# The last tile of a second up projection by seven block products, and where its activations are parted

## The chip, the cores and the metric

The kernel runs on one core of one Trainium2 chip. The metric is device time in microseconds (us), from one launch that computes the whole block. Three runs of the kernel before gave 1013.27, 1013.62 and 1014.18 us; the median is 1013.62 us.

## The reference, cut to what matters

One layer of a streaming encoder on 512 frames of width 1024: a SwiGLU feed-forward network (FFN) with half a step, a token mixer, and a second FFN with half a step. Everything is fp32. The change lies in the second FFN:

```
D_MODEL, SEQ, D_FF = 1024, 512, 2816

def _swiglu(h, w_in, w_out):
    gate, up = jnp.split(h @ w_in, 2, axis=-1)
    return (jax.nn.silu(gate) * up) @ w_out

h = _modulate(x, sh3, s3)
x = x + 0.5 * g3[:, None, :] * _swiglu(h, ffn2_w_in[l], ffn2_w_out[l])
```

The two factors of width 2816 of the up projection, gate and up, are worked in 22 tiles of 128 columns; each tile gives 128 rows of the activation silu(gate) * up, held transposed as 128 partitions by 512 frames.

## The kernel before, in words

**Numbers in two parts.** To keep fp32 accuracy on fp32r matmuls every operand is split into a high part (a cast by ScalarE, ACT) and a low part (a subtraction by VectorE, DVE). A product takes three matmuls: high by high, high by low, low by high (`mm3`, L473). Weights are split by `split_w` (L233, called through `halved`): one cast (L234) and one subtraction (L235) for a tile of 128x1024. Activations are split by `glu_parts` (L915): one cast (L918) and one subtraction (L919) of 128x512. In this text an activation that has been split is "parted".

**Plain tiles.** A plain tile of the up projection (in `by_sevens`, from L1009) takes two weight units, gate and up, each with 8 k-steps of three matmuls of 512 columns: 48 matmuls. `glu` (L907) then applies silu, multiplies and parts the result.

**Tiles by block products.** `seven_products` (L344) computes gate and up of one tile together as a 2x2 block product with seven half-size products in place of eight. Each product is 4 k-steps of three matmuls of 256 columns: 84 matmuls. The order is 1, 2, 6, 7, 5, 4, 3; between them ACT copies partial sums out (L365, L370, L373, L377) and applies silu in two halves (L374, L384), DVE makes three additions (L363) and the last multiplication (`self.mul`, its instruction at L1444). The sums of the inputs (`t7`) are made once; the sums of the weights are made for each tile by `sevenths` (L270): on ACT three casts of 128x1024 and one of 128x512, on DVE three subtractions of 128x1024 and five operations of 128x512. That preparation of tile f+1 is put beside the products of tile f: `side.step()` stands at five places in `seven_products`, and `side.flush()` does the rest after it.

**The second FFN.** `ffn2` (L1263) makes tiles 0 to 2 plainly. `by_sevens` (L974) is called with `SEVEN[1]` = tiles 3 to 20. Then its loop at L1009 makes tile 21 plainly. A generator `parted()` (L1002) parts activations 0 to 7 and 16 to 20 (8 to 15 are in `left` and are parted later); `side.step(3)` at four places beside tile 21 issues twelve of these thirteen. Activations 16 to 21 go to a pool `late` of 12 buffers that takes over the memory of the pool `seven` when the last block product is done (`late_exit`, `late_enter`). A second generator that runs slowly beside the sevens (`ada_more`, 0.12 steps for each step of the first) ends with four matmuls (L885), a copy of their result `rw` (L888) and four transposes (L892).

**The down projection.** `last_down` (L1119) goes through `PLAN`: two heads (output tiles 0 and 1, activations 0 to 7, 24 matmuls of 512 columns each), three tails (activations 16 to 21, 18 matmuls each), three pairs of output tiles by seven block products over activations 0 to 7 (`seven_down`, L1192), five tails, and four pairs over activations 8 to 15. Before matmuls on an activation that isn't parted, it steps the same generator (`self.splits`, L1172). Beside the heads and tails it makes the sums of the activations for the block products (`act_sums`, L1098, instructions at L1102 and L1439, L1440) from the unparted activations 0 to 7 in `self.whole`.

**What sets the order.** The framework fills the queue of each engine ahead of time: among instructions whose inputs it expects to be ready it takes the one that stands first in the program, so work may be drawn ahead into a gap. Three things hold it back. `queued` (L184) ties all ACT instructions issued within it into one chain in the order of the program; the block at L993 holds `seven_products` and `side.flush()`, and the chain goes on from tile to tile. Buffers of one pool and tag (56 in `slots`, four each of `wr`, `wh` and `wl` for weights) are given out in the order in which their first writers stand in the program. And a weight tile's buffers are free only after the matmuls that read them. A load of weights (L139, on the queue of SyncE, SP) starts when its raw buffer `wr` is free; `preload(2)` at L992 calls for the next two loads one tile before the last of the sevens.

Of the kernel before, what the change touches and what calls it, by code (L numbers as in the profile page):

```python
# [25 lines left out]
FT = DFF // P  # L26
EPS = 1e-6
HALF = NT // 2
KPARTS = ((0, 8), (8, 8), (16, 6))
SEVEN = range(6, 21), range(3, 21)  # L30
PAD = 112
SEVENS = 0, 1
PLAN = (("head", 0), ("head", 1), ("tail", 0), ("tail", 1), ("tail", 2), (0, 2), (0, 4), (0, 6), ("tail", 3), ("tail", 4),
# [66 lines left out]
class Block:  # L100
# [325 lines left out]
    def plan_units(self):  # L426
# [4 lines left out]
        def ffn(w1, w2, first, plan, seven=()):  # L431
            for f in range(first, FT):
                if f in seven:
                    self.specs.append(lambda f=f: self.unit_pair(w1, f * P))
                    continue
                cols(w1, f * P)
                cols(w1, DFF + f * P)
            for kind, t in plan:
                if kind in SEVENS:
                    self.specs.append(lambda t=t, k0=8 * kind: self.unit_rows(w2, t, k0))  # L440
                    continue
                for k0, n in (part for i, part in enumerate(KPARTS) if i not in MISSING[kind]):
                    self.specs.append(lambda k0=k0, n=n, t=t: self.unit(w2[k0 * P:(k0 + n) * P, t * P:(t + 1) * P], n))

        ffn(ins["ffn1_w_in"][0], ins["ffn1_w_out"][0], 3, [("all", t) for t in range(KT)], SEVEN[0])
        w = ins["w_in"][0]
# [9 lines left out]
        first = len(self.specs)  # L456
        ffn(ins["ffn2_w_in"][0], ins["ffn2_w_out"][0], 0, PLAN, SEVEN[1])
        del self.specs[first:first + 3]
# [478 lines left out]
    def ffn1(self):  # L937
# [14 lines left out]
        sums.flush()  # L952
        self.by_sevens(act, SEVEN[0], (self.ada_more((1, 2, 3), accs, 0),), 0.3)
        return act
# [19 lines left out]
    def by_sevens(self, act, fs, others, rate, left=()):  # L974

        side, other, self.last_queued = Side(), Side(), None
        other.add(*others)
        both = Rates((side, other), (1, rate))

        def first():  # L980
            yield
            yield
            self.prefetch(1)

        for f in fs:
            w = self.weights7
            if f + 1 in fs:
                side.add(self.next_unit(ahead=0))
            else:
                side.add(first())  # L990
            if f + 2 == fs.stop:
                self.preload(2)  # L992
            with self.queued(mybir.EngineType.Activation, self.last_queued):  # L993
                act.append(self.seven_products(w, both))
                side.flush()
        other.flush()
        self.late_exit()
        self.late_enter(12)
        last = fs[-1] + 1
        self.whole = act[:8]  # L1000

        def parted():  # L1002
            for i in range(last):
                if i not in left:
                    act[i] = self.glu_parts(act[i], i >= 16 if left else 8 <= i < 14)
                    yield

        side.add(parted())
        for f in range(last, FT):  # L1009
            p = []  # L1010
            for _ in range(2):
                u, q = self.next_unit(), self.acc()
                for k in (0, 4):
                    self.dense(q, u, self.h, k0=k, k1=k + 4)
                    side.step(3)
                p.append(q)
            act.append(self.glu(*p, late=bool(left)))
        self.splits = side
# [244 lines left out]
    def ffn2(self, norms):  # L1263
# [13 lines left out]
        side.flush()  # L1277
        self.by_sevens(act, SEVEN[1], (self.ada_more((12, 13), [], 3),), 0.12, range(8, 16))
        self.last_down(act, 8)
# [1209 lines left out]
```

## Time and profile before

| | before |
|---|---|
| median of three runs | 1013.62 us |
| profiled execution, its own time | 1014.92 us |
| its span, first to last instruction | 1013.1 us |
| granted TensorE clock over the span | 0.999 |
| instructions on TensorE (PE) | 7101 matmuls, 7101 weight loads |
| bytes moved by DMA | 130.84 MB, 129 GB/s on the mean |
| DMA engines busy, mean of 16, share of the span by the q1 queue | 42.2% |

A row of the timeline gives the start in us from the start of the span, how long the instruction (or a run of like ones) took, the engine, the line, the operation, the tiles written and read (buffer numbers left out), shapes, the count, and in brackets the idle time of the engine just before it with what ended it. A row of the stages gives the stretch, its length, then the busy time and number of instructions of PE matmul, PE weight load, DVE, ACT and POOL, then the granted clock, the DMA share and GB/s. Matmuls overlap one another, so what one costs in a row of many is the distance between starts, not its own duration.

### The profile page before, as it was taken

What the parts mean: (1) busy time and instruction counts of PE and PEld (TensorE: products, weight loads), DVE (VectorE), ACT (ScalarE), POOL (GpSimd) and SP (SyncE); (2) the same over time, 40 slices, a digit from 0 to 9 for tenths busy, and PEclk for the clock granted to TensorE, in tenths of its full rate; (3) what the DMA queues carried; (4) which work ended last, traced back from release to release, by engine and by line L of the source; (5) the groups of instructions that cost most, each with busy time, mean ns of one, the idle gap of its engine ahead of it and who ended that gap; (6) DMA issues with size and microseconds to landing.
All of it is one profiled execution on the core that took longest, in us unless ns stands there. A gap on an engine that the chain in (4) does not pass through costs nothing.

```text
span 1013.1 us, 18031 instructions
## 1 busy us (share of the span) xinstructions
PE 1001.7 (99%) x7101; PEld 907.7 (90%) x7101; DVE 822.0 (81%) x1461; ACT 527.2 (52%) x954; POOL 30.7 (3%) x74
## 2 busy tenths in 40 slices
PE   7999999999999999999999999999999999999998
PEld 5788999999887889888887888999999999989898
DVE  4778999887797847788987649789998998799984
ACT  4355555556422215658766455375555555655453
POOL 0000000000200000100001012000000000000000
PEclk9999999999999999999999999999999999999999
DMA  9963564434598925412132121212544443323332
GB/s 312 295 208 104 165 208 137 117 102 122 155 323 281 306 65 156 111 47 58 46 75 57 39 63 43 83 43 75 175 121 150 121 131 105 110 83 91 113 104 63
DMA packets 204034, 130.84 MB, mean 129 GB/s; under 512 B 14497, under 2 KB 188590, under 8 KB 203950
## 3 DMA queue, kind: packets, MB, share of 16 engines
q1 hardware_dynamic: 203950, 129.70, 42.2%
q8 instruction: 55, 0.90, 0.4%
q14 instruction: 29, 0.24, 0.1%
HBM read 127.18 MB, written 2.49 MB: 128 GB/s over the span
## 4 chain that ended last, share of the span: by engine, by line
PE 89%; DVE 5%; DMA 2%; SPq 1%; ACT 1%; issue 1%; POOL 0%; DVEq 0%; ACTq 0%
PE pa L360 18%; PE pa L475 14%; PE pa L477 13%; PE pa L476 13%; PE pb L360 13%; PE pa L1207 4%; PE pb L1207 3%; SPq L139 1%; DMA ar<-in_w_ada 1%; PE pb L2175 1%; PE pb L2155 1%; PE pb L475 1%; PE pb L477 1%; PE pb L476 1%; DMA wr<-in_ffn_w_in 1%; PE pb L1712 1%
## 5 line engine op out<-in xcount | busy, mean ns | idle before, releaser
L275 DVE TENSOR_TENSOR wl<-wr,wh 128x1024 fp32r<-128x1024 f32 x120 | 145.8, 1220 | 26.8 <-ACT wh L279 25.8
L279 ACT CAST wh<-wr 128x1024 fp32r<-128x1024 f32 x120 | 123.1, 1051 | 32.9 <-DVE wr L275 18.9
L234 ACT CAST wh<-wr 128x1024 fp32r<-128x1024 f32 (+1 forms) x77 | 76.8, 1006 | 116.8 <-PE pa L476 109.4
L475 PE MATMUL pa<-hh,wh 128*128 128x512 f32 (+1 forms) x309 | 119.4, 386 | 0.0
L235 DVE TENSOR_TENSOR wl<-wr,wh 128x1024 fp32r<-128x1024 f32 (+1 forms) x77 | 89.3, 1165 | 33.4 <-ACT wh L234 33.3
L477 PE MATMUL pa<-hh,wl 128*128 128x512 f32 (+1 forms) x309 | 116.2, 376 | 0.0
L476 PE MATMUL pa<-hl,wh 128*128 128x512 f32 (+1 forms) x309 | 116.1, 376 | 0.0
L475 PE MATMUL pa<-ah,wh 128*128 128x512 f32 (+1 forms) x262 | 97.9, 374 | 0.0
L476 PE MATMUL pa<-al,wh 128*128 128x512 f32 (+1 forms) x262 | 97.5, 372 | 0.0
L477 PE MATMUL pa<-ah,wl 128*128 128x512 f32 (+1 forms) x262 | 97.3, 371 | 0.0
L275 DVE TENSOR_TENSOR wr<-wr,wr 128x512 f32<-128x512 f32 x120 | 82.4, 687 | 1.7
L828 DVE SCALAR_TENSOR_TENSOR aa<-ar,sc,aa 128x512 f32<-128x512 f32 x98 | 73.3, 748 | 8.0 <-DMA ar<-in_w_ada 6.5
L360 PE MATMUL pa<-th,wh 128*128 128x256 f32 x264 | 74.8, 283 | 0.0
L360 PE MATMUL pa<-hh,wh 128*128 128x256 f32 x264 | 74.8, 283 | 0.0
L360 PE MATMUL pa<-tl,wh 128*128 128x256 f32 x264 | 74.7, 283 | 0.0
L360 PE MATMUL pa<-th,wl 128*128 128x256 f32 x264 | 74.7, 283 | 0.0
L360 PE MATMUL pa<-hl,wh 128*128 128x256 f32 x264 | 74.7, 283 | 0.0
L360 PE MATMUL pa<-hh,wl 128*128 128x256 f32 x264 | 74.7, 283 | 0.0
L475 PEld LDWEIGHTS pa<-hh,wh 128*128 128x128 f32 x309 | 58.4, 189 | 10.9 <-issue 2.5
L477 PEld LDWEIGHTS pa<-hh,wl 128*128 128x128 f32 x309 | 58.2, 188 | 10.1
L476 PEld LDWEIGHTS pa<-hl,wh 128*128 128x128 f32 x309 | 58.4, 189 | 8.5
L475 PEld LDWEIGHTS pa<-ah,wh 128*128 128x128 f32 x262 | 49.3, 188 | 10.2 <-ACT wh L234 1.7
(484 smaller groups left out, 2769.1 us busy)
## 6 DMA issues: line engine op xcount, KB each, us to landing
wr<-in_ffn_w_in SPq DMA_DIRECT2D x79, 512.0 KB
ar<-in_w_ada SPq DMA_DIRECT2D x128, 256.0 KB
wr<-in_ffn_w_out SPq DMA_DIRECT2D x32, 512.0 KB
wr<-in_w_in SPq DMA_DIRECT2D x21, 512.0 KB
wr<-in_ffn_w_out SPq DMA_DIRECT2D x16, 384.0 KB
wr<-in_w_out SPq DMA_DIRECT2D x8, 512.0 KB
wr<-in_ffn_w_in SPq DMA_DIRECT2D x8, 384.0 KB
ar<-in_w_ada SPq DMA_DIRECT2D x6, 512.0 KB
```

The source lines that it names most:

```text
L139: return self.nc.sync.dma_start(dst, src)
L234: self.nc.scalar.copy(hi, raw)
L235: self.nc.vector.tensor_tensor(out=lo, in0=raw, in1=hi.bitcast(F32), op=ALU.subtract)
L275: sub = lambda out, x, y: nc.vector.tensor_tensor(out=out, in0=x, in1=y, op=ALU.subtract)
L279: nc.scalar.copy(hi[:, :n], raw[:, :n])
L360: nc.tensor.matmul(z, a[:, j, :], b, start=start and j == 0 and i == 0, stop=j == 3 and i == 2, skip_group_check=not start)
L475: mm(out, wh, xh, start=start, stop=False)
L476: mm(out, wh, xl, start=False, stop=False)
L477: mm(out, wl, xh, start=False, stop=stop)
L828: nc.vector.scalar_tensor_tensor(out=acc, in0=a, scalar=sc, in1=acc, op0=ALU.mult, op1=ALU.add)
L1207: nc.tensor.matmul(z, a[:, j, :], b, start=start and j == 0 and i == 0, stop=j == 3 and i == 2, skip_group_check=not start)
L1712: nc.tensor.matmul(pa[:, ps], kh[:, ps], x[:, ps], start=True, stop=True)
```

## The change

`SEVEN[1]` now ends at tile 21 instead of 20, so the second FFN makes all of tiles 3 to 21 by block products, and `plan_units` loads the weights of tile 21 as one pair (the same two loads of 512 KB). The loop for plain tiles after the sevens finds nothing to do. During tile 21 a generator `begin()` is added to the side work behind `first()`: it yields three times and then parts activations 0 to 3. `first()` yields twice and then splits the weights of head 0. `self.whole` is set before that, because `begin()` replaces entries of `act`. `parted()` skips what is parted already and is left with activations 4 to 7 and 16 to 21; `last_down` steps it. The first FFN calls the same function with tiles up to 20 and keeps its order.

```
-SEVEN = range(6, 21), range(3, 21)
+SEVEN = range(6, 21), range(3, FT)
...
+        def begin():
+            for _ in range(3):
+                yield
+            for i in range(4):
+                act[i] = self.glu_parts(act[i])
+                yield
+
         for f in fs:
             w = self.weights7
...
             if f + 2 == fs.stop:
                 self.preload(2)
+            if f + 1 == FT:
+                self.whole = act[:8]
+                side.add(begin())
             with self.queued(mybir.EngineType.Activation, self.last_queued):
                 act.append(self.seven_products(w, both))
                 side.flush()
...
-        self.whole = act[:8]
+        if last < FT:
+            self.whole = act[:8]
 
         def parted():
             for i in range(last):
-                if i not in left:
+                if i not in left and not isinstance(act[i], tuple):
                     act[i] = self.glu_parts(act[i], i >= 16 if left else 8 <= i < 14)
                     yield
```

## The prediction, made before the changed kernel was run

> **What bounds the kernel now.** I read the page first, then the stages around the change, then the timelines of PE, DVE and ACT there.
>
> ```profile
> span 1013.1 us, 18031 instructions
> PE 1001.7 (99%) x7101; PEld 907.7 (90%) x7101; DVE 822.0 (81%) x1461; ACT 527.2 (52%) x954; POOL 30.7 (3%) x74
> ```
>
> Over the whole span TensorE (PE) hardly ever rests. The stages tell more: tile 19, tile 20, tile 21 with what precedes it, the two heads and three tails, three pairs by block products, five tails, and the first pair of the second set.
>
> ```profile
> core 0: us, PE busy (x) PEld busy (x) DVE busy (x) ACT busy (x) POOL busy (x), PEclk, DMA share, GB/s
> 858.02:868.10 10.08, 10.08 (x87) 10.08 (x86) 8.47 (x13) 5.55 (x10) 0.00 (x0) 1.00 0.37 104
> 868.10:878.18 10.08, 10.08 (x86) 10.03 (x84) 4.85 (x8) 5.25 (x10) 0.00 (x0) 1.00 0.39 108
> 878.18:890.88 12.70, 12.70 (x59) 9.51 (x57) 11.76 (x19) 8.94 (x17) 0.00 (x0) 1.00 0.51 147
> 890.88:914.00 23.12, 23.12 (x104) 19.14 (x102) 21.92 (x39) 11.09 (x16) 0.00 (x0) 1.00 0.23 67
> 914.00:924.08 10.08, 10.08 (x86) 10.08 (x85) 9.71 (x17) 6.03 (x11) 0.00 (x0) 1.00 0.31 94
> 924.08:934.16 10.08, 10.08 (x87) 10.08 (x86) 9.99 (x17) 6.30 (x11) 0.00 (x0) 1.00 0.26 78
> 934.16:944.24 10.08, 10.08 (x87) 10.08 (x86) 9.73 (x18) 5.98 (x11) 0.00 (x0) 1.00 0.60 171
> 944.24:964.66 20.42, 20.42 (x93) 16.89 (x91) 20.13 (x35) 8.89 (x12) 0.00 (x0) 1.00 0.28 80
> 964.66:974.74 10.08, 10.08 (x84) 10.00 (x83) 9.19 (x13) 4.95 (x8) 0.00 (x0) 1.00 0.39 116
> ```
>
> PE is busy in every microsecond of these stages. But from 878 to 965 DVE is too: 9.71 to 9.99 of 10.08 us in the pairs, 20.13 of 20.42 in the five tails. It keeps up only because it is some microseconds ahead. Tile 20 is the last place with room on DVE (4.85 of 10.08), because the plain tile behind it needs little preparation.
>
> **What the change takes from PE.**
>
> ```profile
> 868.10 0.28 PE L360 MATMUL pa<-hh,wh 128*128 128x256 f32 x1
> ...
> 878.27 1.05 PE L885 MATMUL pb<-aa,ones 128*32 128x512 f32 x4
> 879.25 0.50 PE L475 MATMUL pa<-hh,wh 128*128 128x512 f32 x1
> ...
> 890.88 0.39 PE L475 MATMUL pa<-ah,wh 128*128 128x512 f32 x1
> ...
> 896.32 0.39 PE L475 MATMUL pa<-ah,wh 128*128 128x512 f32 x1
> ...
> 968.97 0.28 PE L1207 MATMUL pb<-th,wh 128*128 128x256 f32 x1
> ```
>
> A block-product tile is 84 matmuls in a stage of 10.08 us (858.02 to 868.10): 0.120 us each. Head 0, 24 matmuls from 890.88 to 896.32, gives 0.2267 us for one of 512 columns, so 48 of a plain tile take 10.88 us. PE saves 0.80 us. The four matmuls of L885, 1.07 us of PE from 878.18 to 879.25, stay: the slow generator is one step further in the new tile 21, so they move to between products 6 and 7; their transposes come behind the tile. SP's loads are the same in number and size, and in the same places.
>
> The Trainium skill's page "TensorE: Matmul & The Clock Gate", section "Back-to-back issue gap", gives N/2.4 + 2.5 ns for one matmul, 109 and 216 ns here; by that 84 against 48 would save 1.19 us. The rows above say 120 and 227 ns, and the rows decide.
>
> **What it adds to DVE, and where.** These are DVE's rows from the end of tile 19 to the start of tile 21, and two from later:
>
> ```profile
> 869.38 0.68 DVE L1444 TENSOR_TENSOR af<-sg,up 128x512 f32<-128x512 f32 x1
> 871.25 0.42 DVE L363 TENSOR_TENSOR sg<-pb,z 128x256 f32<-128x256 f32 x1 [1.19 <-PE pb L360]
> 875.71 1.22 DVE L235 TENSOR_TENSOR wl<-wr,wh 128x1024 fp32r<-128x1024 f32 x1 [4.04 <-ACT wh L234]
> 876.86 0.42 DVE L363 TENSOR_TENSOR up<-z 128x256 f32<-128x256 f32 x1
> 877.19 0.42 DVE L363 TENSOR_TENSOR up<-pb,z 128x256 f32<-128x256 f32 x1
> 877.52 2.35 DVE L235 TENSOR_TENSOR wl<-wr,wh 128x1024 fp32r<-128x1024 f32 x2
> 879.79 0.68 DVE L1444 TENSOR_TENSOR af<-sg,up 128x512 f32<-128x512 f32 x1
> ...
> 891.15 0.69 DVE L912 TENSOR_TENSOR af<-sg,pa 128x512 f32<-128x512 f32 x1 [0.96 <-PE pa L477]
> 891.75 0.42 DVE L1102 TENSOR_TENSOR t<-af 128x256 f32<-128x256 f32 x1
> ...
> 965.75 1.23 DVE L275 TENSOR_TENSOR wl<-wr,wh 128x1024 fp32r<-128x1024 f32 x1
> ```
>
> *Work.* In steady state a tile costs DVE 8.47 us, of which its own three additions (0.33 from start to start) and one multiplication (0.60) are 1.6; the preparation of the next pair is thus 6.9, which I round down to 6.7 as runs of instructions overlap. Added: 6.7 for pair 21 and 1.0 for tile 21's three additions. Removed: two weight splits, 1.15 each from start to start. Multiplication and parting of activation 21 cost the same. Net +5.4 us.
>
> *Room.* Tile 20 becomes a steady tile: DVE works 8.47 and idles 1.61 where it idled 5.23. In the new tile 21 there is nothing to prepare but the weights of heads and tails, and they can't begin early: head 0's cast is in ACT's chain behind product 7's copy and silu, and the buffers of head 1's and tail 0's follow its in the program. In the old tile 20 the cast at that place and its subtraction stand at 874.64 (quoted below) and 875.71. One stage of 10.08 and L885's 1.07 later that subtraction starts at 886.86. DVE has finished tile 20 at 869.38 + 0.68 + 10.08 = 880.14, does one addition (0.42), and idles 6.3 us.
>
> Could parting fill this? `begin()` yields three times behind the three steps of `first()`, and there are five steps in a tile; all four partings therefore come in the flush, behind the last silu in ACT's chain. Those of activations 4 to 7 and the sums L1102 wait for buffers of the pool `slots`, given out in program order, so behind those of 0 to 3, which are behind activation 21's own. The trace shows this order holding work back: the sum at 891.75 needs only activations made long before, yet DVE idles 0.96 us for L912, whose buffer comes first. Activations 16 to 20 wait for the pool `seven` to end, after product 4. The old plain tile had none of this: it held DVE busy 11.76 of 12.70 us with partings.
>
> ```profile
> 868.30 0.38 ACT L384 ACTIVATE sg<-pa 128x256 f32<-128x256 f32 x1 [0.61 <-PE pa L360]
> ...
> 874.64 1.04 ACT L234 CAST wh<-wr 128x1024 fp32r<-128x1024 f32 x1
> ...
> 879.95 0.63 ACT L918 CAST ah<-af 128x512 fp32r<-128x512 f32 x1
> ```
>
> *At the border.* The four casts are not beside tile 21, then, but behind it, and head 0 waits for the first. The silu starts 0.20 us after the tile's last matmul slot (868.10 to 868.30) and takes 0.38; the cast takes 0.63; together 1.2 us, less about 0.5 for the transposes that PE has there: 0.7 us. The low part needs one multiplication and one subtraction of 0.6 to 0.7 on DVE more; PE can draw head 1's first matmul in. I price the wait at 0.7 to 1.9. Alone it would leave -0.8 + 1.3 = +0.5 us.
>
> *The account to the end of DVE's busy stretch.* The work that decides last is the subtraction at 965.75, ending at 966.98: it is read by product 7 of the first pair of the second set, whose matmuls start at 968.97. DVE is 2.0 us ahead there. Idle of DVE from 868.10 to 964.66 by the stages: 5.23 + 0.94 + 1.20 + 0.37 + 0.09 + 0.35 + 0.29 = 8.5 us. After: 1.6 + 6.3, and of the 2.3 us behind 890.88 what is left. The 0.96 us wait at 891.15, and a few others for PE, go once DVE is the late one; I take 0.3, between 0 and 2.3. DVE is then later by 5.4 + 8.2 - 8.5 = 5.1 us, 2.0 are covered, and PE has to wait until **+3.1 us**. This holds the border wait and the 0.8 saved: PE waits 3.9 in all, part of it at the border, the rest in products 6 and 7 of the pairs. Behind 974.74 nothing is given back, since PE is busy throughout. With the idle left at 0 and 2.3 the sum is 2.8 and 4.8; if half the 2.0 us lead can't be used, 1.0 more; if the sums of the work are 1.0 too high or the framework draws work behind this subtraction, 1.0 less.
>
> The profiled execution took 1014.92 us, 1.8 more than its span and 1.30 more than the median. I add 3.1 to span (1016.2) and median alike: **1016.7 us**. A measurement of this kernel tells about 0.2%, 2.0 us, from no change.
>
> **Rivals.**
>
> *PE alone decides: faster by 0.8 to 0.9.* PE is busy 99%, so what it saves is saved. The Trainium skill's page "Perfetto Trace Analysis", section "Identifying the Most-Contended Engine", has it so: the engine with the highest occupancy is the one to improve. For it: PE doesn't wait once between 868 and 975 now. Against it: the stages show DVE at 96 to 99% over 30 us, and DVE gets 5.4 us more. It would need 3 us of partings within DVE's 6.3 us gap, which the chain and the buffer order forbid. 1012.8 us; chance 0.10.
>
> *Only the border wait counts.* The account is 2.5 us too high because the framework, finding DVE late, sets work back that PE doesn't need before 975 (updates of xT, later partings), or because DVE's lead is larger than the one row shows. Then -0.8 + 1.0 to 2.3: +0.2 to +1.5, 1014.2 us at +0.6; chance 0.25.
>
> *DVE's debt decides*: the forecast, slower than before, from the point where the debt (5.1) is over the lead (2.0). 1016.7, between 1015.6 and 1018.4; chance 0.57.
>
> *The heads starve as well.* If ACT and DVE alternate between activations 0 to 7 and 16 to 20, an activation comes every 1.2 us (twice 0.60) while head 0 eats one in 0.68 (3 x 0.2267). If PE's queue can't interleave head 1, eight of them cost 8 x 0.52 = 4.2 us on top of the 1.2: +4.6, 1018.2 or a little over; chance 0.05.
>
> *The change doesn't do what it says* in the sense that nothing is parted beside the tile: that is in the forecast. Its opposite, four partings (2.4 us) in the gap, would bring the debt to 2.7 and the end to about +0.7, within the second rival. A gain of over 2.0 us has no mechanism that I can find: 0.03.
>
> **How the numbers follow.** Slower by over 0.2% takes most of the forecast (0.55 of its 0.57) and the starving heads: 0.60. Within 0.2%: 0.37. Faster: 0.03. The range 1013.4 to 1018.5 leaves out the first rival below and the worst of the last one above. The forecast's own range is 1015.6 to 1018.4.
>
> **What would show it.** Right: in tile 21 DVE busy under half of the first 8 us; the casts of activations 0 to 3 directly behind the last silu; PE's first wait at head 0, 0.7 to 1.9 us; more PE waits, for DVE's weight subtractions or sums, in the first four pairs; no difference in any tile before 868. Wrong: DVE subtractions L919 in the gap of tile 21; no PE wait in the pairs; head 0 starting without a wait; a span that differs before 868.

## The result, and the profile after

The changed kernel takes 1017.81 us (median of 15 runs, 1015.88 to 1020.36); the kernel before, on the same chip in turn with it, 1014.51 us (median of 15 runs, 1013.21 to 1018.07). The ratio is 1.0032, with a 95% interval of 1.0025 to 1.0039: slower by about 3.3 us.

The first part of the page of the changed kernel has the span and each engine's busy time:

```profile
span 1018.5 us, 18100 instructions
PE 1004.1 (99%) x7137; PEld 910.8 (89%) x7137; DVE 826.3 (81%) x1470; ACT 529.9 (52%) x961; POOL 30.6 (3%) x74
```

PE, DVE and ACT look as they did. The execution that was profiled took 1020.36 us, the longest of the fifteen, so its times are for reading the mechanism, and the medians for its size. The stages tell where it went. The seven rows are those that the prediction shows of the kernel before (tile 19, tile 20, tile 21, heads and tails, three pairs, five tails, first pair of the second set), except that the three pairs stand in one row; the eighth is the first 8 us of tile 21.

```profile
core 0: us, PE busy (x) PEld busy (x) DVE busy (x) ACT busy (x) POOL busy (x), PEclk, DMA share, GB/s
858.75:868.83 10.08, 10.08 (x87) 10.08 (x85) 8.46 (x13) 5.56 (x10) 0.00 (x0) 1.00 0.37 104
868.83:878.91 10.08, 10.08 (x87) 10.08 (x85) 8.45 (x13) 5.55 (x10) 0.00 (x0) 1.00 0.36 106
878.91:891.91 13.00, 11.79 (x94) 10.55 (x92) 6.59 (x11) 7.52 (x15) 0.00 (x0) 1.00 0.32 93
891.91:917.54 25.63, 25.16 (x103) 20.31 (x103) 23.97 (x46) 12.73 (x22) 0.00 (x0) 0.93 0.28 82
917.54:949.65 32.11, 30.95 (x254) 30.46 (x252) 32.11 (x53) 19.34 (x35) 0.00 (x0) 1.00 0.33 97
949.65:970.08 20.43, 20.43 (x93) 16.90 (x91) 19.75 (x38) 9.57 (x14) 0.00 (x0) 1.00 0.35 101
970.08:980.16 10.08, 10.08 (x86) 10.08 (x85) 9.57 (x15) 5.17 (x9) 0.00 (x0) 1.00 0.38 106
878.91:886.91 8.00, 8.00 (x63) 7.03 (x62) 2.40 (x4) 2.58 (x7) 0.00 (x0) 1.00 0.34 99
```

Tile 21 with its border is 0.30 us longer (12.70 before), heads and tails 2.51 (23.12), the three pairs 1.88 (30.23). Behind the pairs nothing changes: five tails 20.43 against 20.42, the first pair of the second set 10.08 both times. The remaining 0.73 us lies before tile 21 (878.91 against 878.18), and all of it already before tile 19 (858.75 against 858.02); PE's instructions up to there are the same, and executions vary by as much (in the control of the experiments, whose edit lies behind 914, the plain tile 21 starts at 878.35, in the kernel before at 879.25).

PE's waits from 860 to 1010, grouped by the instruction that waited and the one that released it, as total, count and longest; in the kernel before this view is empty:

```profile
PE pa L475 <- ACT ah L918: 1.2, 1, 1.2
PE pa L1218 <- DVE wl L275: 0.7, 1, 0.7
PE pa L476 <- DVE al L919: 0.5, 1, 0.5
PE pb L1218 <- ACT wh L279: 0.4, 1, 0.4
```

Four waits, at two places. The first place is the border of tile 21 and head 0, in PE's timeline:

```profile
890.25 0.46 PE L892 MATMUL pb<-ident,rw 64*128 64x64 f32 x4
891.91 0.73 PE L475 MATMUL pa<-ah,wh 128*128 128x512 f32 x2 [1.21 <-ACT ah L918]
893.11 0.50 PE L476 MATMUL pa<-al,wh 128*128 128x512 f32 x1 [0.46 <-DVE al L919]
...
893.92 0.59 PE L476 MATMUL pa<-al,wh 128*128 128x512 f32 x1
894.32 0.63 PE L477 MATMUL pa<-ah,wl 128*128 128x512 f32 x1
...
897.30 0.43 PE L475 MATMUL pa<-ah,wh 128*128 128x512 f32 x1
```

Head 0 waits for the high part of its first activation, does the two matmuls that it can, and waits again for the low part. Then its matmuls come 0.43 us apart (894.32, 894.74, ...) in place of 0.23. The stage view of just that stretch gives the granted clock:

```profile
893.92:897.30 3.38, 3.38 (x9) 2.61 (x8) 3.38 (x7) 3.38 (x8) 0.00 (x0) 0.50 0.95 284
```

Half the clock for 3.4 us costs this execution 1.6 us (eight matmuls at 0.2 us more). It isn't in every execution. Of the fifteen runs, seven have a mean clock of 0.999 or 1.0 and a median of 1017.08 us; the eight with 0.997 or 0.998 have 1018.54.

The second place is the first of the three pairs, in PE's timeline:

```profile
917.54 0.28 PE L1218 MATMUL pa<-ah,wh 128*128 128x256 f32 x1
...
921.39 0.38 PE L1218 MATMUL pb<-th,wh 128*128 128x256 f32 x1 [0.44 <-ACT wh L279]
...
925.49 0.39 PE L1218 MATMUL pa<-ah,wl 128*128 128x256 f32 x1 [0.72 <-DVE wl L275]
```

And DVE's weight subtractions there, in the kernel after and then in the kernel before:

```profile
920.16 1.23 DVE L275 TENSOR_TENSOR wl<-wr,wh 128x1024 fp32r<-128x1024 f32 x1
...
921.96 1.21 DVE L275 TENSOR_TENSOR wl<-wr,wh 128x1024 fp32r<-128x1024 f32 x1
...
924.22 1.21 DVE L275 TENSOR_TENSOR wl<-wr,wh 128x1024 fp32r<-128x1024 f32 x1
```

```profile
911.10 2.35 DVE L275 TENSOR_TENSOR wl<-wr,wh 128x1024 fp32r<-128x1024 f32 x2
...
915.10 1.23 DVE L275 TENSOR_TENSOR wl<-wr,wh 128x1024 fp32r<-128x1024 f32 x1 [0.15 <-ACT wh L279]
```

The first two are the later weights of pair 1 (for products 5 and 6, then 7 and 3), the third is the first weights of pair 2. Before, the two were ready when the pairs began at 914.00 (911.10 + 2.35 = 913.45), and DVE itself waited for ACT ahead of the third. After, all three come while the pair runs, one behind the other. The PE row at 925.49 is a matmul of pair 2: the framework had drawn it in among those of pair 1, and in PE's queue it holds up all behind it. In the kernel before it was not drawn in. There the same matmul comes behind all of pair 1, 10.31 us after the pairs' start:

```profile
924.31 0.28 PE L1207 MATMUL pa<-ah,wl 128*128 128x256 f32 x1
```

The third subtraction sums the matter up in one number. Let its **lag** be its end less the start of the pairs: 915.10 + 1.23 - 914.00 = 2.33 us before, 924.22 + 1.21 - 917.54 = 7.89 after. The experiments below are read by it.

### The profile page after: what moved, and what is told of

Read it like the earlier page. It is cut to its first block, busy times and chain, and to the rows that moved or that the text cites. A ratio compares the mean times of both kernels' runs of the same rounds, so it can differ in the third digit from the quotient of the medians.

```text
span 1018.5 us, 18100 instructions
## 1 busy us (share of the span) xinstructions
PE 1004.1 (99%) x7137; PEld 910.8 (89%) x7137; DVE 826.3 (81%) x1470; ACT 529.9 (52%) x961; POOL 30.6 (3%) x74
## 5 line engine op out<-in xcount | busy, mean ns | idle before, releaser
L275 DVE TENSOR_TENSOR wl<-wr,wh 128x1024 fp32r<-128x1024 f32 x123 | 149.1, 1219 | 26.8 <-ACT wh L279 25.9
L279 ACT CAST wh<-wr 128x1024 fp32r<-128x1024 f32 x123 | 125.7, 1051 | 25.9 <-DVE wr L275 21.5
L235 DVE TENSOR_TENSOR wl<-wr,wh 128x1024 fp32r<-128x1024 f32 (+1 forms) x75 | 86.9, 1163 | 36.0 <-ACT wh L234 35.8
L475 PE MATMUL pa<-hh,wh 128*128 128x512 f32 (+1 forms) x293 | 113.0, 386 | 0.0
L477 PE MATMUL pa<-hh,wl 128*128 128x512 f32 (+1 forms) x293 | 110.0, 375 | 0.0
L476 PE MATMUL pa<-hl,wh 128*128 128x512 f32 (+1 forms) x293 | 109.9, 375 | 0.0
L360 PE MATMUL pa<-th,wh 128*128 128x256 f32 x272 | 77.1, 283 | 0.5 <-ACT z L365 0.5
L475 PEld LDWEIGHTS pa<-hh,wh 128*128 128x128 f32 x293 | 55.4, 189 | 9.5 <-issue 1.6
L477 PEld LDWEIGHTS pa<-hh,wl 128*128 128x128 f32 x293 | 55.2, 188 | 9.6
L476 PEld LDWEIGHTS pa<-hl,wh 128*128 128x128 f32 x293 | 55.4, 189 | 7.9
```

Source lines behind the costliest of these rows:

```text
L235: self.nc.vector.tensor_tensor(out=lo, in0=raw, in1=hi.bitcast(F32), op=ALU.subtract)
L275: sub = lambda out, x, y: nc.vector.tensor_tensor(out=out, in0=x, in1=y, op=ALU.subtract)
L279: nc.scalar.copy(hi[:, :n], raw[:, :n])
L360: nc.tensor.matmul(z, a[:, j, :], b, start=start and j == 0 and i == 0, stop=j == 3 and i == 2, skip_group_check=not start)
L475: mm(out, wh, xh, start=start, stop=False)
L476: mm(out, wh, xl, start=False, stop=False)
```

## The experiments

Ratios are against the kernel before, run in turn on the same chip, with 95% intervals; each kernel was executed 5 to 12 times. "Waits" are by how much the starts of neighbouring matmuls on PE lie further apart than 0.120 us (0.227 for 512 columns), summed over 905 to 935, or the part of it where it says so. Theory A is the forecast's: DVE is late by its added work and by the gap in tile 21, and PE pays what is over DVE's lead.

**Four partings inside tile 21.** The three empty steps of `begin()` go, it calls for head 0's weights itself, and `first()` isn't added for the last tile, so that activations 0 to 3 are parted within tile 21 and not behind it.

```
         def begin():
-            for _ in range(3):
-                yield
             for i in range(4):
+                if i == 2:
+                    self.prefetch(1)
                 act[i] = self.glu_parts(act[i])
                 yield
...
-            else:
+            elif f + 1 < FT:
                 side.add(first())
```

> The changed kernel, but the four partings of activations 0 to 3 are issued at steps 1 to 4 inside tile 21 (head 0's weights still split at step 3), so they can run in DVE's idle stretch there. Theory A (DVE's debt): the border wait goes, and 2.4 us of DVE's work moves into the idle stretch; debt 5.1 to 6.5 less 2.4, less the lead of 2.0: +0.7 to +2 us against the kernel before; waits in the first pair by block products stay. Theory B (only the wait at head 0 and the half clock behind it cost): nothing is left but PE's saving, -0.8 us.

Measured: 1016.28 us, ratio 1.0020 (1.0011 to 1.0029). Head 0 starts at 890.21, right behind L892: the border wait is gone, and with it the half clock. The waits in the first pair grew, to 2.4 us from 1.8. Two of them:

```profile
917.36 0.39 PE L1218 MATMUL pa<-th,wh 128*128 128x256 f32 x1 [0.55 <-ACT wh L279]
...
918.62 0.38 PE L1218 MATMUL pb<-th,wh 128*128 128x256 f32 x1 [0.75 <-ACT wh L279]
```

Measured from the start of tile 20, and against the run without `begin()` below (the changed kernel without the half clock), PE came to the pairs 1.8 us earlier and DVE to the end of the third subtraction only 1.4, so the lag rose to 8.37. Of the 1.7 us of border wait 0.6 was paid in the pairs. That the border is the whole loss is refuted; the 2.0 us that are left lie at the upper end of what A gave.

**Eight partings inside tile 21.** The same with two at each of four steps.

```
         def begin():
-            for _ in range(3):
-                yield
-            for i in range(4):
-                act[i] = self.glu_parts(act[i])
+            for step in ((0, 1), (2, 3), (), (4, 5), (6, 7)):
+                if not step:
+                    self.prefetch(1)
+                for i in step:
+                    act[i] = self.glu_parts(act[i])
                 yield
...
-            else:
+            elif f + 1 < FT:
                 side.add(first())
```

> As the last one, but eight partings (0 to 3 at steps 1 and 2, 4 to 7 at steps 4 and 5 of tile 21). Theory A: 4.8 us of work in the idle stretch, the debt is 0.3 to 1.7 and under the lead of 2.0, so only PE's saving is left: -0.8 us against the kernel before (between -1.2 and +0.3). Theory B: the same -0.8, no better than with four.

Measured: 1013.55 us, ratio 0.9992 (0.9983 to 1.0000), the lowest ratio of the study, with an interval that reaches to no gain. DVE's idle time in tile 21 falls from 6.4 to 3.9 us, the border wait is gone, and the lag is down to 7.07 us. One wait of 0.95 us with its restart is left, for that same subtraction:

```profile
919.68 0.39 PE L1219 MATMUL pa<-ah,wl 128*128 128x256 f32 x1 [0.69 <-DVE wl L275]
```

That wait eats what PE saves. From the start of tile 20 to the first pair of the second set PE takes 96.77 us here and 96.56 in the kernel before, so the trace doesn't show the median's gain at the place of the change. The same stretch is 101.25 us in the changed kernel, and 99.76 in the next run, which had no half clock.

**No `begin()`.** No partings are added beside tile 21; `parted()` does all of them behind it.

```
-                side.add(begin())
```

> The changed kernel without begin(): all fourteen partings are left to the generator that the heads step. Theory A: no difference from the changed kernel, +3.3 us against the kernel before (+2.5 to +4), because activation 21's buffer and DVE's work are the same. Theory C (ACT's chain holds the four casts, the rest doesn't matter): the casts come free and start earlier; +1 us or less.

Measured: 1017.10 us, ratio 1.0028 (1.0018 to 1.0037), as the changed kernel. The same four waits, of the same lengths (1.21, 0.46, 0.44, 0.72 us), and a lag of 7.90. The four partings "beside" the last tile are not beside it: the generator does nothing that its absence wouldn't.

**Plain tile, four partings.** The kernel before, with one parting a step in place of three beside its plain tile 21 (the calls share this line; the first FFN keeps three).

```
-                    side.step(3)
+                    side.step(1 if left else 3)
```

> The kernel before with a plain tile 21, but four partings beside it in place of twelve: the second half of the change alone. Theory A: eight partings, 4.8 us of DVE, move behind the tile, where DVE has 2.0 us of lead: +1.5 to +3 us against the kernel before. Theory D (the block products of tile 21 and their preparation are what costs): within 0.5 us of the kernel before.

Measured: 1014.23 us, ratio 1.0001 (0.9991 to 1.0010). A expected 1.5 us or more and missed; the rival, that only the block products' preparation costs, held here. The lag is 6.24, and PE waits 0.1 us. So DVE's lead was larger than the 2.0 us of the forecast.

**DVE's work alone, in three doses.** The kernel before, with the low-part subtraction of some activations repeated, which adds work to DVE and nothing else.

```
-        nc.vector.tensor_tensor(out=al[:, ts], in0=a[:, ts], in1=ah[:, ts].bitcast(F32), op=ALU.subtract)
+        for _ in range(1 + again):
+            nc.vector.tensor_tensor(out=al[:, ts], in0=a[:, ts], in1=ah[:, ts].bitcast(F32), op=ALU.subtract)
```

> The kernel before with three of these subtractions (activations 5 to 7) made twice: 1.8 us more on DVE. Theory A: under the lead of 2.0 us and DVE's small idle stretches, so no cost, -0.3 to +0.5 us against the kernel before. A bound without any lead would give +1.8 us.

> The kernel before, with nine of the low-part subtractions of parting (activations 3 to 7 and 16 to 19) made twice: 9 x 0.6 = 5.4 us more on DVE beside the old tile 21 and the heads, and nothing else. Theory A (DVE's debt over a lead of 2.0 us): +1.5 to +3.4 us against the kernel before, with PE waits for DVE at the first pairs by block products. Theory B (only the wait at head 0 and the half clock behind it cost): 0 to +0.5 us.

Measured: three repeats, 1014.78 us, ratio 1.0005 (0.9996 to 1.0014); nine, 1014.62 us, ratio 1.0005 (0.9996 to 1.0014). Nine repeats are the 5.4 us that the forecast gave the change, and they cost nothing: A, as it was put, failed a second time. The third subtraction, with nine repeats:

```profile
913.78 0.28 PE L1209 MATMUL pa<-ah,wh 128*128 128x256 f32 x1
```

```profile
918.55 1.22 DVE L275 TENSOR_TENSOR wl<-wr,wh 128x1024 fp32r<-128x1024 f32 x1
```

The lag is 918.55 + 1.22 - 913.78 = 5.99, and PE doesn't wait. Of the 5.4 us only 3.66 came through. DVE idles 2.5 us between 878 and the third subtraction in the kernel before, in six waits for PE and ACT of up to 0.96 us, and 0.3 us here: work that comes late doesn't wait again. What is left must be under DVE's lead. That gave theory A its present form, to be tried by a third dose: PE waits from a lag of about 6.1 us on, so the lead of the kernel before is 6.1 - 2.3 = 3.8 us. (That lead holds in a queue with the matmul drawn in, as in the nine repeats, where it starts 6.23 us after the pairs. By its own queue, with that matmul at 10.31, the kernel before has 8.0 us at this subtraction.)

> The kernel before with each of nine low-part subtractions of activations (3 to 7 and 16 to 19) done three times: DVE gets 18 x 0.60 = 10.8 us more ahead of the three pairs. Theory A, as it stands after seven runs: one instruction decides, DVE's subtraction for the first weights of the second pair. In the kernel before it ends 2.33 us after the pairs start; waits were seen from about 6.1 on, so the lead is 3.8 us. Nine repeats moved it to 5.99, using up DVE's idle time on the way; the next nine have no idle time left to use and move it by their full 5.4 to 11.4. Loss 5.3 us (4.5 to 6), ratio 1.0052. Rival D: work added to DVE costs nothing, only the block products' own preparation in the last tile does: 0 (under 0.8), as nine repeats gave.

Measured: 1020.70 us, ratio 1.0061 (1.0049 to 1.0073), 6.2 us where 5.3 (4.5 to 6) was expected: once idle time and lead are used up, DVE's added work is paid, and the rival is refuted. That it costs just its own time isn't shown: the stretch from tile 20 to the second set is 5.5 us longer than before, but 1.6 of that is a stretch of half the clock behind the wait, and the one execution of six with a mean clock of 1.0 took 1018.69 us, 4.7 over the kernel before. The place was another than the expectation's. PE paid at head 1, whose weights stand behind the repeats in DVE's queue, and the pairs then ran with a lag of 6.21 and 0.1 us of waits:

```profile
PE pa L477 <- DVE wl L235: 3.5, 1, 3.5
```

**PE kept busy at the border.** The changed kernel with 14 matmuls of 256 columns, whose result nobody reads, between tile 21 and head 0.

```
         other.flush()
+        if fs.stop == FT:
+            pz = self.aux()
+            for _ in range(14):
+                self.nc.tensor.matmul(pz[:, :HALF], w[3][0][:, 0, :], self.h[4][0][:, HALF:], start=True, stop=True)
```

> The changed kernel with fourteen matmuls of 256 columns (1.7 us, into a bank that nobody reads) between tile 21 and head 0, so that PE is not idle at the border. If the half clock behind the border comes of PE's idle time, it doesn't appear. Theory A: PE comes to the first pair earlier and waits there for DVE instead; no more than 1 us is won against the changed kernel, +2.3 to +3.6 us against the kernel before. Theory B: the half clock's 1.6 us is won, +1.5 us or less.

Measured: 1017.51 us, ratio 1.0034 (1.0021 to 1.0046). No wait at the border and no half clock in its profile; the lag is 7.98 and the waits in the first pair 1.9 us. No gain shows, though the interval is too wide to see the 0.8 us that the half clock costs on the mean of the fifteen runs (1.5 us in eight of them). The matmuls without use take the time of the wait. That the border and the half clock are the whole loss, which would have left 1.5 us or less here, is refuted again.

**The changed kernel with less DVE work.** Nine low-part subtractions are left out; the high parts stand in for them.

```
+        if less:
+            return ah, ah
```

> The changed kernel with nine low-part subtractions (activations 4 to 7 and 16 to 20) left out; their high parts are read in place of the low parts, so the output is not the reference's. DVE has 5.4 us less ahead of the pairs, the last tile and the border are as in the changed kernel. Theory A: the subtraction that decides ends 7.89 - 5.4 = 2.5 us after the pairs start, within the lead, so the waits in the first pair go; the border wait of 1.2 + 0.5 us stays. Left over against the kernel before: -0.8 + 1.2 + 0.5 = +0.9, or up to +2.5 in executions where the clock drops to half behind the border. Ratio 1.0009 to 1.0025. Rival E, the border and the clock behind it are all of it: as the changed kernel, +3.3, ratio 1.0032.

Measured: 1015.96 us, ratio 1.0016 (1.0007 to 1.0025), within the 0.9 to 2.5 us that A gave. The lag is 3.20 and PE doesn't wait in the pairs. What is left is the border, and in the profiled execution the half clock behind it (0.43 us from 890.77 on):

```profile
890.18 1.22 PE L475 MATMUL pa<-ah,wh 128*128 128x512 f32 x2 [1.69 <-ACT ah L918]
891.20 0.63 PE L476 MATMUL pa<-al,wh 128*128 128x512 f32 x1
```

So about half of the 3.3 us goes when DVE's work goes; the other half is the border and the clock, net of the 0.8 us that PE saves. The halves don't add up freely: with the border alone removed, above, a part of its price came back in the pairs.

**Towards a better kernel.** First, eight partings as above, and in the pairs the weights' step ahead of the updates; the same move alone in the kernel before is its control.

```
         product(zc, 2, True)
+        side.step()
         update(t, l, sa[:, l])
         update(t, l, zc)
         next(between, None)
-        side.step()
```

> The changed kernel with eight partings beside tile 21 (as in the run with eight, -0.9 us) and, in the down projection's pairs, the step of the next pair's weight preparation that follows product 2 put ahead of the three updates that stood before it. Theory A: the subtraction that PE waited 0.85 us for comes 1.0 us earlier on DVE (two updates of 0.48 and 0.43 for the parting in between go behind it), so that wait goes: -0.8 - 0.9 = -1.7 us (-1.2 to -2.0), ratio 0.9983. Rival: the updates free the buffers that the next products write, so their delay costs PE what the earlier weights save: -0.9 or less, ratio 0.9992.

> The kernel before with only that step moved ahead of the updates in the pairs. It is the control for the run before: PE waits nowhere in these pairs, so there is nothing to gain, 0 (within 0.6 us). If the updates hold PE's buffers: slower by 0.5 to 2.

Measured: 1014.24 us, ratio 1.0001 (0.9993 to 1.0010), and the control 1014.19 us, ratio 1.0002 (0.9993 to 1.0010). The lag fell to 5.95 as meant and the wait at that subtraction went, but two others took its place, in the second pair and in the third, both for ACT, here with the idle time that the view gives:

```profile
PE pa L1219 <- ACT z L1223: 0.4, 1, 0.4
PE pa L1219 <- ACT wh L279: 0.2, 1, 0.2
```

With their restarts they are 0.5 and 0.7 us (from the starts at 925.63 and 936.58). The gain of 1.7 us was not there. The rival, that the gain is paid back by what was put off, fits; that the updates held PSUM buffers, as it was worded, was not isolated.

Second, eight partings, and two of the four subtractions in each sum of activations on GpSimd.

```
-            sub(t12[:, l], a[:, r], a[:, l])
+            pool(t12[:, l], a[:, r], a[:, l])
...
-            sub(t34[:, l], b[:, r], a[:, r])
+            pool(t34[:, l], b[:, r], a[:, r])
```

> The changed kernel with eight partings beside tile 21, and two of the four subtractions of each sum of activations in the down projection (the two that read activations alone, 128x256) on GpSimd, which is busy 3% of the span. Ahead of the first pair that takes 8 x 0.335 = 2.7 us from DVE. In the run with eight partings the subtraction that decides ended 7.07 us after the pairs start, about 1.0 over what the pairs can bear. Theory A: 2.7 less brings it to 4.4, PE waits nowhere in the pairs, and the saving on PE stays whole: -1.9 us (-1.3 to -2.3) against the kernel before, ratio 0.9981. Rival F: DVE is late throughout from tile 21 to the tails, and a wait that is removed at one place comes back at the next, as in the run with the moved step: 0 to -0.9. Rival G: GpSimd takes over twice as long for one of them (1.16 to 1.30 us for 128x512 in the kernel before, so about 0.65 against 0.42), the sums come late or DVE's instructions beside them get longer: 0 to +2.

Measured: 1020.01 us, ratio 1.0051 (1.0037 to 1.0064), 5.7 us slower by the medians where 1.9 faster was expected: the last of the rivals, and more than it allowed. The timelines of GpSimd, ACT and DVE:

```profile
886.14 0.74 POOL L1119 TENSOR_TENSOR t<-af 128x256 f32<-128x256 f32 x1 [220.52 <-PE pa L360]
886.84 1.72 POOL L1119 TENSOR_TENSOR t<-af,af 128x256 f32<-128x256 f32 x1
...
897.86 10.35 POOL L1119 TENSOR_TENSOR t<-af 128x256 f32<-128x256 f32 x1 [4.46 <-ACT wh L234]
908.17 4.38 POOL L1119 TENSOR_TENSOR t<-af,af 128x256 f32<-128x256 f32 x1
```

```profile
912.59 0.62 ACT L1452 CAST th<-t 128x512 fp32r<-128x512 f32 x1 [2.72 <-POOL t L1119]
```

```profile
887.88 1.23 DVE L919 TENSOR_TENSOR al<-af,ah 128x512 fp32r<-128x512 f32 x1
889.03 1.75 DVE L235 TENSOR_TENSOR wl<-wr,wh 128x1024 fp32r<-128x1024 f32 x1
890.71 1.23 DVE L919 TENSOR_TENSOR al<-af,ah 128x512 fp32r<-128x512 f32 x1
```

Spans on GpSimd are rough, but DVE's aren't: beside GpSimd a low part takes 1.23 us in place of 0.68, a weight subtraction 1.75 in place of 1.22. And the sums came late, as ACT's wait shows. By the distances between its matmuls PE lost 0.9 us in head 0, 1.6 in the first pair and 2.3 in the second set, there with a stretch of half the clock behind it.

**All by the lag.** The lag and the waits on PE from 905 to 935, worked out alike in each trace (of the last run, whose sums come from GpSimd, below):

| kernel | lag, us | waits, us |
|---|---|---|
| before; with the moved step | 2.33; 2.33 | 0; 0 |
| three repeats | 2.61 | 0 |
| changed, nine subtractions fewer | 3.20 | 0 |
| eight partings and moved step | 5.95 | 0.56, none for this subtraction |
| nine repeats | 5.99 | 0 |
| eighteen repeats | 6.21 | 0.10 |
| plain tile, four partings | 6.24 | 0.10 |
| eight partings | 7.07 | 1.02 |
| changed | 7.89 | 1.79 |
| no `begin()` | 7.90 | 1.80 |
| PE kept busy | 7.98 | 1.92 |
| four partings | 8.37 | 2.42 |

From 6.1 us on, the waits are the lag less 6.1, to within 0.2 us. The number has a plain cause: in every kernel of the table with a lag of 5.95 or more, 52 matmuls, 6.24 us, stand between the pairs' start and the drawn-in one. So the fit says that this matmul's wait is the last to end in the first pair, and is no second proof that DVE's work costs time. In the kernels with a lag of up to 3.20 that matmul isn't drawn in, and neither is it in the run with GpSimd: there the lag is 7.15, and PE doesn't wait for this subtraction at all (its wait there is for ACT). The limit of 6.1 thus belongs to the order that the framework chose. How much of the 1.8 us the changed kernel would have waited in the old order, no run shows.

## Why the prediction was right, and where it was not

*PE's saving, 0.80 us: right.* A block-product tile is again 84 matmuls 0.120 us apart, and with eight partings inside the tile, where no wait stands at the border, head 0 starts 21.80 us after tile 20 in place of 22.78. That is 0.98 us less, a little over the forecast; the kernel's time gives it only as 0.8 us (0 to 1.7), with the wait in the pairs inside it. The Trainium skill's figure for one matmul by itself, from the page "TensorE: Matmul & The Clock Gate", section "Back-to-back issue gap", would make the saving 1.19; this interval can't tell the two apart, the rows can.

*DVE's room: right.* It idles 10.08 - 8.45 = 1.6 us in tile 20, as forecast. Tile 21 on DVE:

```profile
880.20 0.68 DVE L1455 TENSOR_TENSOR af<-sg,up 128x512 f32<-128x512 f32 x1
882.06 0.42 DVE L363 TENSOR_TENSOR sg<-pb,z 128x256 f32<-128x256 f32 x1 [1.18 <-PE pb L360]
887.69 1.22 DVE L235 TENSOR_TENSOR wl<-wr,wh 128x1024 fp32r<-128x1024 f32 x1 [5.21 <-ACT wh L234]
```

The idle time is 1.18 + 5.21 = 6.4 us (forecast 6.3), ended by head 0's cast, and DVE is busy 2.40 of the first 8 us.

*The order behind the tile: right.* ACT casts the activations in one run behind the last silu. What was forecast to be useless, `begin()`, is: without it the time is the same.

```profile
890.98 0.38 ACT L384 ACTIVATE sg<-pa 128x256 f32<-128x256 f32 x1
891.25 1.13 ACT L918 CAST ah<-af 128x512 fp32r<-128x512 f32 x2
```

*The border wait, 0.7 to 1.9 us: right in its place, cause and size* (1.21 + 0.46 = 1.7). Its consequence for the clock wasn't foreseen: 1.6 us in the profiled execution.

*The account: right in kind, near in sum by luck, wrong in place and in both of its terms.* The step that failed is the choice of the subtraction at 965.75 as the one that decides. It stands in the first pair of the second set; PE waited in the first pair of the first set only, and by the five tails the debt is gone. I had measured the lead at the end of DVE's busy stretch, on the ground that DVE hardly idles up to there. But PE has deadlines all along the stretch, and the first that is missed makes PE wait, which pays the debt for all that follow. At the subtraction that decides, the terms are these, from the stages up to its end:

```profile
868.10:878.18 10.08, 10.08 (x86) 10.03 (x84) 4.85 (x8) 5.25 (x10) 0.00 (x0) 1.00 0.39 108
878.18:916.33 38.15, 38.15 (x180) 30.98 (x179) 35.66 (x61) 21.79 (x36) 0.00 (x0) 1.00 0.37 107
```

```profile
868.83:878.91 10.08, 10.08 (x87) 10.08 (x85) 8.45 (x13) 5.55 (x10) 0.00 (x0) 1.00 0.36 106
878.91:925.43 46.52, 43.74 (x248) 37.16 (x246) 38.45 (x68) 25.88 (x46) 0.00 (x0) 0.96 0.30 85
```

DVE needs 56.60 us where it needed 48.23, 8.4 more, and not 5.1. Its work is 46.90 against 40.51, 6.4 more and not 5.4: two half updates of xT (0.48 and 0.47) and half an activation's parting (0.42) now stand ahead of that subtraction. Its idle time is 9.7 against 7.7, 2.0 more, where I had 0.3 less. I had counted on the idle time in the heads to shrink to 0.3; it is 1.7, most of it one wait for a weight buffer that PE, late itself, sets free:

```profile
903.91 0.84 ACT L234 CAST wh<-wr 128x768 fp32r<-128x768 f32 x1 [5.81 <-PE pa L476]
```

```profile
904.78 0.96 DVE L235 TENSOR_TENSOR wl<-wr,wh 128x768 fp32r<-128x768 f32 x1 [1.56 <-ACT wh L234]
```

The lead there is 3.8 us, with the matmul drawn in as the changed kernel has it, and not 2.0; the rows of the kernel before couldn't show this deadline, since the framework sets the order anew for each kernel. So the debt and the lead were both too small, and 8.4 - 3.8 = 4.6 us is what this execution lost from tile 21 to the end of the pairs (0.30 + 2.51 + 1.88 = 4.7; the two are the same loss, read from DVE's side and from PE's), 1.6 of it the clock. Without the half clock that is 3.0, near the +3.1 of the forecast because two errors cancel, which is luck. (One sum of the range was off besides: with 2.3 us of idle time left the account gives 5.1, not 4.8. It bears on the upper end alone.)

*The rivals.* PE alone decides: refuted, the kernel is slower. The Trainium skill, on the page "Perfetto Trace Analysis", section "Identifying the Most-Contended Engine", says to improve the engine with the highest occupancy first. Here that is PE, at 99% (90% by its weight loads, which the section names for TensorE, against 81% on DVE), and 0.8 us taken from it by work given to DVE cost 3.3; the trace speaks against the rule where a second engine has only microseconds of lead. Only the border wait counts: refuted by the four partings inside the tile, which remove it and keep 2 us of the loss. Heads that starve: not in the changed kernel, where no head waits after its first activation; eighteen repeats show that it can be.

*What would make it wrong.* Of the signs listed, two came in part: PE waits in the first of four pairs and not in all, and the span before 868 differs by the 0.73 us that such executions differ by.

## What to carry to other kernels

Where one engine is always busy and a second is nearly so, list the second's deadlines along its whole busy stretch and take the lead at each; the first that is missed decides, and the end of the stretch can be blind to it. A deadline is the place of the reading instruction in the other engine's queue, and it can move when the kernel changes: here one came 4 us earlier. Added work on the second engine is paid only over its small idle times and that lead, so 5.4 us can cost nothing and the next 5.4 about all of it. Work put "beside" a tile counts only if it can start there: look at the chain, the buffers and the step at which the generator first does something.

## What the runs showed of the hardware

*Half the clock behind a short wait.* Waits of 1.21 and 0.46 us within 2.4 us were followed by 3.4 us at a granted clock of 0.50. In the run without `begin()` the profile has the same two waits and no such stretch (its clock is 1.0 over the span); waits of 1.69, 3.45 and 2.07 us brought it in the runs with nine subtractions fewer, with eighteen repeats and with GpSimd; one of 1.34 us in the run with GpSimd, and all shorter single ones, did not. The Trainium skill, page "TensorE: Matmul & The Clock Gate", section "What's actually happening", has the clock fall after an idle window of about 3.4 us and says that the window runs freely. The stretch's length and its coming and going agree with such a window, and so does the trace's record of the clock, in which the full clock lasts 884.05 us ahead of the stretch and 119.47 us behind it, 259 and 35 times the 3.413 us of the stretch; but PE never idled for 3.4 us at a stretch in the changed kernel, so the idle time that is enough is shorter than the page says. Which share of a window it takes, no run here settles.

*The restart.* The matmul that follows the first one behind a wait comes 0.22 us later instead of 0.12 (921.39 to 921.61, 925.49 to 925.71): each wait costs 0.1 us beyond its length.

*GpSimd beside a busy DVE.* In the run with sums on GpSimd both slow down: a subtraction of 128x256 on GpSimd took 0.74 us at first and 1.18 and 1.72 behind that, and DVE's there took 1.4 to 1.8 times their time (1.75 for 1.22, 1.23 for 0.68). From 898 on it was GpSimd alone that suffered: one subtraction lasted 10.35 us, while DVE's low parts beside it took their usual 0.69. The Trainium skill, page "GPSIMD Engine Reference", section "1. Specifications", says that GpSimd shares its SBUF interfaces with VectorE and meets contention from DVE instructions with two SBUF inputs, as these subtractions are. The trace agrees that they contend; who pays changed within it.
